# Layer norms with weight and bias as two fused VectorE operations, and gating issued two pairs ahead of its projection

## The chip, the cores and the metric

The kernel runs on one core of one Trainium2 chip. The metric is the device time of one execution in microseconds (us); smaller is better. A core has five engines that the profile names PE (TensorE; its weight loads are PEld), DVE (VectorE), ACT (ScalarE), POOL (GpSimd) and SP (SyncE, which here issues all DMAs). Each engine works through its own instruction list in order and waits where an operand, or the place for a result, is not ready.

## The reference

A two-layer backbone over 1024 latent tokens and 256 context tokens, 1024 features, all in float32. The last layer drops the context tokens, so layer 0 works on ten tiles of 128 tokens and layer 1, in the parts that matter here, on eight.

```
def layer_norm(x, g=None, b=None):
    mu = mean(x, -1); var = mean((x - mu)**2, -1)
    y = (x - mu) * rsqrt(var + 1e-5)
    return y if g is None else y * g + b
# one layer, with shifts, scales and gates from the conditioning vector:
u  = layer_norm(x) * (1 + scale0) + shift0
y  = four mixers of u @ w_in, each group-normed and gated
x1 = layer_norm(ALPHA * x + gate0 * (y @ w_out), ln1_g, ln1_b)
u2 = layer_norm(x1) * (1 + scale1) + shift1
x  = layer_norm(ALPHA * x1 + gate1 * conv_ffn(u2), ln2_g, ln2_b)
```

## The kernel before

Activations for a product lie feature-major in SBUF as two parts, `k.uh` (rounded) and `k.ul` (the rest); `mm3` (L1018 to L1024) makes one product out of three matmuls (L1021 to L1023). A layer runs the four mixers, then `mix_out`, then `ffn`.

`mix_out` (L1127) goes over pairs of token tiles in the order 2, 4, 0, 6, 8 (layer 1: 2, 4, 0, 6). `prep(g0)` gates one pair: DMAs bring the mixers' outputs `yt` and gates `gt` (L1137, L1140), PE transposes them (L1145), ACT and DVE scale and gate them into `yT` (L1148, L1149, L1153), ACT writes `k.uh` (L1156) and POOL `k.ul` (L1157). `out(t)` then does one tile: 48 matmuls with `wo` into two PSUM banks, DVE applies the mixer's gate and adds the residual (`mt`, L1165, L1166), `norm_out` (L1199) normalizes with weight `rg` and bias `rb` into `xt` and stores it, `ln_apply` (L991) normalizes again without weight or bias, and `to_u` (L998) transposes (L1004), modulates (`tum`, L1007 on DVE, L1008 on ACT) and writes `k.uh` on ACT (L1009) and `k.ul` on POOL (L1010) for the feed-forward part. In the loop, `prep` of the next pair is written just ahead of the two `out` of the current one. The last pair uses DVE where the others use POOL.

A layer norm with weight and bias (`norm_out`) is: `ln_stats` (L979; DVE bn_stats and bn_aggr, L983 and L984, a square root on ACT, L985, a reciprocal on DVE, L986, and the product -mean*rstd on DVE, L987), one pass on ACT (L995), the product with the weight (L1204) and the sum with the bias (L1205). In `mix_out` both of these are on POOL; at the end of `ffn` (L1278) the product is on DVE and the sum on POOL.

At the end of `ffn` (L1269 to L1281) each token tile gets its last product in two banks; the second half is added into `facc` (L1277), `norm_out` makes the layer's output from the first bank and that half, and in layer 0 `next_u` (L1266) makes the input of layer 1 with `ln_apply` and `to_u`.

The instruction lists are not in the order of the code: the tile framework schedules with its own timeline, so a change of an operation can move others on every engine.

Of the kernel before, what the change touches and what calls it, by code (L numbers as in the profile page):

```python
# [10 lines left out]
F32=mybir.dt.float32  # L11
# [3 lines left out]
ALU=mybir.AluOpType  # L15
# [5 lines left out]
def rwkv_consts():  # L21
    c={}
# [5 lines left out]
    c['rwmask']=np.stack([mf,mb],1)          # [128,2,128]  # L28
# [10 lines left out]
def mr_consts():  # L39
# [3 lines left out]
    mk=np.zeros((128,2,128),np.float32)   # [j,dir,i]  # L43
    mk[:,0]=np.where(i[:,None]>i[None,:],-1e30,0); mk[:,1]=np.where(i[:,None]<i[None,:],-1e30,0)
    c['mmask']=mk
    # selection for token-major gathers: rows 0-7 wi, 32-39 wk, 64-71 em ; cols (dir,12)
# [5 lines left out]
    # decay broadcast: lhsT [8,(ft,dir),128]  # L52
# [5 lines left out]
    # block-diagonal rows [8 rows,(dir) , h', i]  # L58
# [26 lines left out]
def dft_consts(L):  # L85
    """two-stage real DFT of length 2L, n=128*n1+n2, k=R*m+r, R=2L/128"""
# [10 lines left out]
    F0=np.zeros((128,4,64))   # re0, reH, im0(row0=nyquist), imH  # L97
    F0[:,0]=np.cos(a0);F0[:,1]=np.cos(aH);F0[:,2]=-np.sin(a0);F0[:,2,0]=(-1.0)**n2;F0[:,3]=-np.sin(aH)
    I0=np.zeros((128,4,128))  # B0 from re, B0 from im, BH from re, BH from im
# [36 lines left out]
class Eng:  # L136
    """elementwise ops on DVE or on Pool"""
    def __init__(s,nc,pool): s.nc=nc; s.e=nc.gpsimd if pool else nc.vector; s.pool=pool
    def tt(s,out,a,b,op): s.e.tensor_tensor(out=out,in0=a,in1=b,op=op)
    def axpy(s,out,a,sc,b,op=ALU.add,tmp=None):   # a*sc op b  # L140
# [5 lines left out]
def stage_a(K,E,x,H,CW,ptag):  # L146
    """x: view [128,H,CW] (n1 = token tile). returns accessor re(r), im(r) for r=0..H"""
# [29 lines left out]
def fwd_slot(K,cs,dst_re,dst_im,slot,H,pre,pim,qre=None,qim=None):  # L177
    """matmuls of one slot: re part from (pre,pim), im part from (qre,qim)"""
# [10 lines left out]
def fft_conv(K,Ksp,x,out,H,CW):  # L189
    """x view [128,H,CW], Ksp DRAM AP [128,H,2,CW]; out callback(par(0/1), AP [128,H//2,CW] time values)"""  # L190
# [18 lines left out]
    BB=p.tile([128,2*H,CW],F32,tag="hE",name="BB")   # re r -> r (0..H), im r -> H+r  # L209
# [20 lines left out]
    # g: [128, comp(re,im), r, par, CW]  # L230
# [10 lines left out]
    # a4: even +re B4, odd -im B4  # L241
# [14 lines left out]
def hyena_filter(K,l,L,Ksp):  # L256
    """Ksp DRAM tile [2 order][128,H,2,256]"""
# [89 lines left out]
def seg_conv(k,dst,src,w,ctx=True):  # L347
    """three-tap conv of a padded feature-major tile; w = (prev, mid, next, bias) columns"""
# [18 lines left out]
def kparts(k,D,ft,t,kk):  # L367
    """keys (or normalized keys) to the groups of wrk: r | k of even heads, kk of odd ones | the other way round | kk"""
# [7 lines left out]
def rwkv_front(k,l,pv,pvr,last):  # L376
    """projections, token shift, key normalization, gate and bonus of the RWKV group"""
# [52 lines left out]
def rwkv(K,l,pv,last,p1,p2,p3):  # L430
    """Chunked scan, 64 tokens a chunk, both directions at once, two chunks of each a step.  Even heads keep (b,SA,S) on partitions
    0-63 and (k,V) on 64-127, odd heads the other way round."""
# [610 lines left out]
def later(k,fn=None):  # L1043
    """what follows a projection on the tensor engine is put behind the next projection"""
    p,k.pend=k.pend,fn
    if p: p()
# [398 lines left out]
```

## Time and profile before

| | |
|---|---|
| Time, median of 3 runs | 4327.93 us (4318.99 to 4331.74) |
| Span of the profiled execution | 4332.8 us |
| Median against that span | 4.9 us less |
| `mix_out` in layer 0, layer 1 | 1242 to 1422, 3424 to 3578 us |
| End of `ffn` in layer 0, layer 1 | 2304 to 2404, 4286 to 4333 us |

The profiled execution has no time of its own beside its span; the span lies 1.1 us above the slowest of the three runs. Sums of this text are made against the span, and the 4.9 us are taken off at the end. The stretches in the table are read from the timeline: from the first matmul with `wo` to the last `k.uh` that the feed-forward part waits for, and from the first bn_stats of the last norm to the last `tum` of layer 0, or to the end of the program.

### The profile page before, as it was taken

The numbers are of one execution on the slowest core, as the hardware profiler recorded it, in microseconds if no ns is written. First come the engines' busy times: TensorE is split into PE (matmuls) and PEld (weight loads), VectorE is DVE, ScalarE is ACT, GpSimd is POOL, SyncE is SP. The second block draws the span as 40 slices with busy tenths as digits, with TensorE's granted clock in tenths as the row PEclk, the third lists the DMA queues.
The fourth block names the chain that finished last, engine by engine and source line by source line (L and its number), as shares of the span: only waits on it lengthen the run. The fifth ranks groups of instructions, "written<-read, shape, count | busy, mean of one in ns | idle before, by whom it ended". The sixth has DMA issues, their size and how long they took to land.

```text
span 4332.8 us, 65427 instructions
## 1 busy us (share of the span) xinstructions
PE 3976.9 (92%) x24976; PEld 3226.9 (74%) x24976; DVE 2644.4 (61%) x5384; ACT 1462.4 (34%) x2909; POOL 1094.6 (25%) x2204
## 2 busy tenths in 40 slices
PE   6999999689979999999996899997899879999997
PEld 3878877566657888888884688885666758888885
DVE  5656665889766544444448555776889664444446
ACT  4333233554344211111124443344544342112112
POOL 3230023566535000000033330033666340000004
PEclk6999999799989999999998999996899789999999
DMA  4235553444343111111113235553333331111112
GB/s 164 72 102 173 158 152 110 114 145 121 116 134 122 45 39 35 44 40 35 38 36 114 83 103 153 171 160 96 123 111 102 125 102 54 45 43 54 44 49 97
DMA packets 477141, 414.18 MB, mean 96 GB/s; under 512 B 48827, under 2 KB 443285, under 8 KB 474011
## 3 DMA queue, kind: packets, MB, share of 16 engines
q1 hardware_dynamic: 476826, 409.99, 31.1%
q8 instruction: 197, 3.23, 0.3%
q14 instruction: 118, 0.96, 0.1%
HBM read 323.65 MB, written 86.25 MB: 95 GB/s over the span
## 4 chain that ended last, share of the span: by engine, by line
PE 49%; DVE 11%; ACT 3%; issue 3%; DMA 3%; POOL 3%; SPq 0%; POOLq 0%; ACTq 0%; DVEq 0%
PE bank L1021 8%; PE bank L1023 8%; PE bank L1022 8%; PE dbank L1021 6%; PE dbank L1022 6%; PE dbank L1023 6%; DMA xt<-x 1%; DVE bst L983 1%; POOL ul L1157 1%; DVE facc L1204 1%; PE bank L186 1%; PE bank L187 0%; DMA wst<-in_w_out 0%; DVE G L530 0%; DVE XL L558 0%
## 5 line engine op out<-in xcount | busy, mean ns | idle before, releaser
L1021 PE MATMUL dbank<-uh,wh 128*128 128x512 f32 (+1 forms) x2120 | 764.4, 370 | 9.5 <-ACT tmpB L398 5.5
L1022 PE MATMUL dbank<-ul,wh 128*128 128x512 f32 (+1 forms) x2120 | 760.0, 368 | 0.0
L1015 DVE TENSOR_TENSOR wl<-wst,wh 128x1024 fp32r<-128x1024 f32 x146 | 188.9, 1295 | 491.4 <-ACT wh L1014 342.0
L1023 PE MATMUL dbank<-uh,wl 128*128 128x512 f32 (+1 forms) x2120 | 480.9, 367 | 0.0
L1021 PEld LDWEIGHTS dbank<-uh,wh 128*128 128x128 f32 x2120 | 401.1, 189 | 85.8 <-ACT ztok L1113 6.1
L1022 PEld LDWEIGHTS dbank<-ul,wh 128*128 128x128 f32 x2120 | 401.3, 189 | 68.4 <-issue 0.8
L1023 PEld LDWEIGHTS dbank<-uh,wl 128*128 128x128 f32 x2120 | 366.2, 188 | 70.6 <-issue 1.1
L1232 POOL MEMSET fz<- 128x1 f32 x132 | 7.3, 99 | 1441.4 <-DVE fc L1247 1441.2
L1021 PE MATMUL bank<-uh,wh 128*128 128x512 f32 (+1 forms) x920 | 337.8, 375 | 11.4 <-ACT uh L1009 11.4
L1263 DVE TENSOR_TENSOR facc<-facc,bank 128x512 f32<-128x512 f32 x324 | 222.1, 687 | 204.8 <-PE bank L1023 204.8
L1022 PE MATMUL bank<-ul,wh 128*128 128x512 f32 (+1 forms) x920 | 337.9, 375 | 4.1 <-POOL ul L1010 3.6
L1021 PE MATMUL bank<-wdh,gh 128*128 128x512 f32 x792 | 315.2, 400 | 19.2 <-DVE facc L1277 11.1
L1022 PE MATMUL bank<-wdl,gh 128*128 128x512 f32 x792 | 310.5, 392 | 3.4 <-DVE wdl L1015 3.4
L1023 PE MATMUL bank<-wdh,gl 128*128 128x512 f32 x792 | 248.7, 393 | 0.0
L1014 ACT ACTIVATE wh<-wst 128x1024 fp32r<-128x1024 f32 x146 | 154.6, 1059 | 226.2 <-PE dbank L1022 157.7
L1014 ACT ACTIVATE wdh<-wst 128x1024 fp32r<-128x1024 f32 x46 | 48.7, 1061 | 524.8 <-PE bank L1023 427.8
L557 POOL TENSOR_TENSOR lt<-LM,XL 128x48 f32<-128x48 f32 (+26 forms) x620 | 187.4, 302 | 121.7 <-ACT XL L551 51.1
L558 POOL TENSOR_TENSOR XL<-XL,lt 128x48 f32<-128x48 f32 (+26 forms) x620 | 205.9, 332 | 47.8
L1023 PE MATMUL bank<-uh,wl 128*128 128x512 f32 (+1 forms) x920 | 212.6, 373 | 0.0
L1021 PEld LDWEIGHTS bank<-uh,wh 128*128 128x128 f32 x920 | 176.2, 192 | 42.9 <-ACT uh L1009 12.2
L1022 PEld LDWEIGHTS bank<-ul,wh 128*128 128x128 f32 x920 | 176.0, 191 | 36.1 <-POOL ul L1010 4.3
L1021 PEld LDWEIGHTS bank<-wdh,gh 128*128 128x128 f32 x792 | 149.9, 189 | 59.2 <-DVE facc L1277 11.9
(480 smaller groups left out, 8283.0 us busy)
## 6 DMA issues: line engine op xcount, KB each, us to landing
wst<-in_ffn_w_up SPq DMA_DIRECT2D x88, 512.0 KB
adaw<-in_ada_w SPq DMA_DIRECT2D x160, 256.0 KB
wst<-in_w_in SPq DMA_DIRECT2D x58, 512.0 KB
wst<-in_ffn_w_down SPq DMA_DIRECT2D x46, 512.0 KB
df<-in_c_F SPq DMA_DIRECT2D x10, 1344.0 KB
xt<-x SPq DMA_DIRECT2D x26, 512.0 KB
df<-in_c_I SPq DMA_DIRECT2D x8, 1344.0 KB
rkk<-wrk SPq DMA_DIRECT2D x10, 1024.0 KB
```

Source lines behind the costliest of these rows:

```text
L186: mm(dst_re,F[:,i],pre(slot),start=True,stop=False); mm(dst_re,F[:,i+1],pim(slot),start=False,stop=True)
L557: e.tensor_tensor(out=t_,in0=LM[:,j,j+1:32].unsqueeze(2).to_broadcast([128,n,m]),in1=X[h][:,j:j+1,0:m].to_broadcast([128,n,m]),op=A.mult)
L558: e.tensor_tensor(out=X[h][:,j+1:32,0:m],in0=X[h][:,j+1:32,0:m],in1=t_,op=A.add)
L983: for h in range(2): nc.vector.bn_stats(out=st[:,h],in_=x[h])
L1014: k.nc.scalar.activation(out=h,in_=st,func=ACTF.Copy)
L1015: k.nc.vector.tensor_tensor(out=lo,in0=st,in1=h,op=ALU.subtract)
L1021: mm(ps,lh,rh,start=(i==0),stop=False)
L1022: mm(ps,lh,rl,start=False,stop=False)
L1023: for i,((lh,ll),(rh,rl)) in enumerate(pairs): mm(ps,ll,rh,start=False,stop=(i==n-1 and more is None))
L1157: nc.gpsimd.tensor_tensor(out=k.ul[:,fs,c],in0=yT,in1=k.uh[:,fs,c],op=ALU.subtract)
L1204: e[0].tensor_tensor(out=y,in0=y,in1=g,op=ALU.mult)
L1263: else: tt(out=d,in0=d,in1=ps,op=ALU.add)
```

## The change

`norm_out` no longer calls `ln_apply`. `ln_stats` returns rstd and the mean themselves, without L987, and two operations on DVE do the rest: (x - mean) * weight, and that times rstd plus the bias. At the end of `ffn` the first of them is split in two halves, since the first half of the tile still lies in PSUM. ACT's pass and POOL's two operations are gone from every such norm, and so is the choice of engine. `prep` is called for two pairs ahead of the loop, and in the loop for the pair after the next. Comments were taken out as well, and one line was added, so that line numbers from L987 on are higher by one in the changed kernel.

```
-def ln_stats(k,x):
+def ln_stats(k,x,raw=False):
...
     nc.vector.reciprocal(out=mv[:,2:3],in_=mv[:,2:3])
+    if raw: return mv[:,2:3],mv[:,0:1]
     nc.vector.scalar_tensor_tensor(out=mv[:,3:4],in0=mv[:,0:1],scalar=-1.0,in1=mv[:,2:3],op0=ALU.mult,op1=ALU.mult)
...
-            norm_out(k,t,m,xt,bc['g'],bc['b'],D['x1'],eng)
+            norm_out(k,t,m,xt,bc['g'],bc['b'],D['x1'])
...
-        prep(order[0])
+        prep(order[0]); prep(order[1])
...
-            if i+1<len(order): prep(order[i+1])
-            else: ep.close()
+            if i+2<len(order): prep(order[i+2])
+            elif i+2==len(order): ep.close()
...
-def norm_out(k,t,x,y,g,b,dst,eng=None):
-    nc=k.nc
-    ln_apply(k,y,x)
-    e=eng if isinstance(eng,tuple) else (eng or nc.gpsimd,)*2
-    e[0].tensor_tensor(out=y,in0=y,in1=g,op=ALU.mult)
-    e[1].tensor_tensor(out=y,in0=y,in1=b,op=ALU.add)
+def norm_out(k,t,x,y,g,b,dst):
+    nc=k.nc; stt=nc.vector.scalar_tensor_tensor; hs=[slice(h*512,h*512+512) for h in range(2)]
+    parts=isinstance(x,list)
+    r,m=ln_stats(k,x if parts else [x[:,h] for h in hs],True)
+    for o,i,gg in zip([y[:,h] for h in hs],x,[g[:,h] for h in hs]) if parts else [(y,x,g)]: stt(out=o,in0=i,scalar=m,in1=gg,op0=ALU.subtract,op1=ALU.mult)
+    stt(out=y,in0=y,scalar=r,in1=b,op0=ALU.mult,op1=ALU.add)
     nc.sync.dma_start(dst[t*128:t*128+128],y)
...
-                norm_out(k,t,v,m,g,b,out if last else k.Dn['x'],(nc.vector,nc.gpsimd))
+                norm_out(k,t,v,m,g,b,out if last else k.Dn['x'])
```

On DVE in `mix_out` of layer 0, from the first tile's sum with the residual on, before (`bst` and `bmv` are the statistics, `rm` the gate's row) and then in the changed kernel:

```order
L1166 SCALAR_TENSOR_TENSOR mt<-xt,mt 128x1024
L983 BN_STATS bst<-mt 128x6 x2
L984 BN_AGGR bmv<-bst 128x2
L1165 TENSOR_TENSOR mt<-bank,rm_12708 128x512
L986 RECIPROCAL bmv<-bmv 128x1
L987 SCALAR_TENSOR_TENSOR bmv<-bmv 128x1
L1165 TENSOR_TENSOR mt<-bank,rm_12708 128x512
L1166 SCALAR_TENSOR_TENSOR mt<-xt,mt 128x1024
L983 BN_STATS bst<-xt 128x6 x2
L983 BN_STATS bst<-mt 128x6 x2
L984 BN_AGGR bmv<-bst 128x2 x2
```

```order
L1167 SCALAR_TENSOR_TENSOR mt<-xt,mt 128x1024
L983 BN_STATS bst<-mt 128x6 x2
L984 BN_AGGR bmv<-bst 128x2
L1166 TENSOR_TENSOR mt<-bank,rm_12755 128x512
L1205 SCALAR_TENSOR_TENSOR xt<-mt,bmv,rg 128x1024
L986 RECIPROCAL bmv<-bmv 128x1
L1154 TENSOR_TENSOR yT<-yT,gt 128x512
L1206 SCALAR_TENSOR_TENSOR xt<-xt,bmv,rb 128x1024
L983 BN_STATS bst<-xt 128x6 x2
L984 BN_AGGR bmv<-bst 128x2
L986 RECIPROCAL bmv<-bmv 128x1
L988 SCALAR_TENSOR_TENSOR bmv<-bmv 128x1
```

The first tile's norm now follows its statistics at once on DVE, ahead of the second tile's sum with the residual; before, the statistics of its result (bst<-xt) stood behind the second tile's L1166. A gating product of a later pair (L1154) stands between the two fused operations.

On ACT at the same place, behind the gating of the second pair, before and then in the changed kernel:

```order
L985 ACTIVATE bmv<-bmv,eps_74 128x1
L995 ACTIVATE xt<-mt,bmv 128x1024
L985 ACTIVATE bmv<-bmv,eps_74 128x1 x2
L995 ACTIVATE mt<-xt,bmv 128x1024
L995 ACTIVATE xt<-mt,bmv 128x1024
L1008 ACTIVATE tum<-dbank,modc 128x128 x4
L1009 ACTIVATE uh<-tum 128x8x128
L985 ACTIVATE bmv<-bmv,eps_74 128x1 x2
L995 ACTIVATE mt<-xt,bmv 128x1024
L995 ACTIVATE xt<-mt,bmv 128x1024
```

```order
L985 ACTIVATE bmv<-bmv,eps_74 128x1
L1149 ACTIVATE yT<-dbank,pvm_1661 128x256 x4
L1157 ACTIVATE uh<-yT 128x4x256
L985 ACTIVATE bmv<-bmv,eps_74 128x1
L1149 ACTIVATE yT<-dbank,pvm_1661 128x256 x2
L996 ACTIVATE mt<-xt,bmv 128x1024
L1157 ACTIVATE uh<-yT 128x4x256
L985 ACTIVATE bmv<-bmv,eps_74 128x1
L1009 ACTIVATE tum<-dbank,modc 128x128 x4
L1010 ACTIVATE uh<-tum 128x8x128
```

ACT's passes into xt are gone, and the gating of the third pair (yT and uh<-yT) has moved up to the first two tiles' norms; before, its first rows came only behind the second tile's `tum`.

On DVE at the end of layer 1, where the last eight tiles are normed, from the first tile's statistics on, before and then in the changed kernel:

```order
L984 BN_AGGR bmv<-bst 128x2
L983 BN_STATS bst<-facc 128x6
L986 RECIPROCAL bmv<-bmv 128x1
L984 BN_AGGR bmv<-bst 128x2
L987 SCALAR_TENSOR_TENSOR bmv<-bmv 128x1
L983 BN_STATS bst<-bank 128x6
L986 RECIPROCAL bmv<-bmv 128x1
L987 SCALAR_TENSOR_TENSOR bmv<-bmv 128x1
L1277 TENSOR_TENSOR facc<-facc,bank 128x512
L1204 TENSOR_TENSOR facc<-facc,ln_g 128x1024
L983 BN_STATS bst<-facc 128x6
L1204 TENSOR_TENSOR facc<-facc,ln_g 128x1024
```

```order
L984 BN_AGGR bmv<-bst 128x2
L983 BN_STATS bst<-facc 128x6
L1205 SCALAR_TENSOR_TENSOR facc<-bank,bmv,ln_g 128x512
L1205 SCALAR_TENSOR_TENSOR facc<-facc,bmv,ln_g 128x512
L986 RECIPROCAL bmv<-bmv 128x1
L984 BN_AGGR bmv<-bst 128x2
L983 BN_STATS bst<-bank 128x6
L1206 SCALAR_TENSOR_TENSOR facc<-facc,bmv,ln_b 128x1024
L1205 SCALAR_TENSOR_TENSOR facc<-bank,bmv,ln_g 128x512
L1205 SCALAR_TENSOR_TENSOR facc<-facc,bmv,ln_g 128x512
```

Each tile has three fused operations in place of one product, the reciprocal stands behind the first two of them, and nothing of the norm is left on POOL.

## Rows read from the trace of the kernel before

**Rows 1.** The page: busy us of each engine (share of the span) and instructions.
```profile
PE 3976.9 (92%) x24976; PEld 3226.9 (74%) x24976; DVE 2644.4 (61%) x5384; ACT 1462.4 (34%) x2909; POOL 1094.6 (25%) x2204
```

**Rows 2.** Busy time by stretch: us, busy per engine (instructions), PEclk, DMA share, GB/s.
```profile
1242.00:1422.00 180.00, 161.39 (x719) 129.01 (x719) 117.24 (x203) 82.57 (x136) 85.99 (x37) 0.94 0.37 120
2304.00:2404.00 100.00, 59.57 (x235) 38.42 (x233) 82.68 (x168) 58.10 (x103) 45.17 (x23) 0.78 0.27 93
3424.00:3578.00 154.00, 125.30 (x546) 98.95 (x547) 93.38 (x164) 65.41 (x107) 67.24 (x29) 0.90 0.35 113
4286.00:4332.00 46.00, 21.64 (x78) 13.90 (x76) 36.97 (x57) 13.45 (x24) 18.83 (x8) 0.82 0.23 92
```

**Rows 3.** PE's waits, 1242 to 1422: us in total, times, longest.
```profile
PE bank L1021 <- ACT uh L1156: 29.1, 6, 20.3
```

**Rows 4.** PE's waits, 3420 to 3580, same columns.
```profile
PE bank L1021 <- ACT uh L1156: 12.4, 5, 4.2
```

**Rows 5.** Timeline of PE, both layers: start, us, instruction [idle before].
```profile
1242.30 0.77 PE L1021 MATMUL bank<-wo,uh 128*128 128x512 f32 x1 [20.34 <-ACT uh L1156]
...
1280.51 1.03 PE L1004 MATMUL dbank<-ident,mt 128*128 128x128 f32 x8
...
1415.23 1.09 PE L1004 MATMUL dbank<-ident,mt 128*128 128x128 f32 x8 [1.28 <-ACT mt L995]
...
3463.16 1.04 PE L1004 MATMUL dbank<-ident,mt 128*128 128x128 f32 x8
...
3571.18 1.09 PE L1004 MATMUL dbank<-ident,mt 128*128 128x128 f32 x8 [1.29 <-ACT mt L995]
```

**Rows 6.** Groups by line on DVE, 1266 to 1390: busy us, mean ns | idle before.
```profile
L1166 DVE SCALAR_TENSOR_TENSOR mt<-xt,mt 128x1024 f32<-128x1024 f32 x8 | 17.6, 2199 | 0.1
L1153 DVE TENSOR_TENSOR yT<-yT,gt 128x512 f32<-128x512 f32 x9 | 12.1, 1350 | 3.7 <-ACT yT L1148 3.6
...
L1165 DVE TENSOR_TENSOR mt<-bank,rm 128x512 f32<-128x512 f32 x16 | 10.5, 683 | 12.3 <-PE bank L1023 12.3
...
L987 DVE SCALAR_TENSOR_TENSOR bmv<-bmv 128x1 f32<-128x1 f32 x15 | 8.7, 600 | 0.2
```

**Rows 7.** Timeline of DVE around the projection of layer 0.
```profile
1265.75 0.16 DVE L987 SCALAR_TENSOR_TENSOR bmv<-bmv 128x1 f32<-128x1 f32 x1
...
1294.74 0.69 DVE L1153 TENSOR_TENSOR yT<-yT,gt 128x512 f32<-128x512 f32 x1
1295.35 3.38 DVE L1166 SCALAR_TENSOR_TENSOR mt<-xt,mt 128x1024 f32<-128x1024 f32 x1
...
1318.93 1.23 DVE L1166 SCALAR_TENSOR_TENSOR mt<-xt,mt 128x1024 f32<-128x1024 f32 x1
...
1399.08 1.22 DVE L1204 TENSOR_TENSOR xt<-xt,rg 128x1024 f32<-128x1024 f32 x1
```

**Rows 8.** Groups by line on POOL, 1242 to 1422.
```profile
L1157 POOL TENSOR_TENSOR ul<-yT,uh 128x1024 fp32r<-128x1024 f32 x10 | 24.9, 2494 | 32.5 <-ACT uh L1156 32.5
L1010 POOL TENSOR_TENSOR ul<-tum,uh 128x1024 fp32r<-128x1024 f32 x8 | 21.1, 2642 | 20.1 <-ACT uh L1009 12.0 <-DVE mt L1165 8.1
L1205 POOL TENSOR_TENSOR xt<-xt,rb 128x1024 f32<-128x1024 f32 x8 | 21.1, 2635 | 0.5
L1204 POOL TENSOR_TENSOR xt<-xt,rg 128x1024 f32<-128x1024 f32 x8 | 19.1, 2383 | 30.5 <-ACT xt L995 30.5
```

**Rows 9.** Groups by line on DVE, 2304 to 2404.
```profile
L1204 DVE TENSOR_TENSOR facc<-facc,ln_g 128x1024 f32<-128x1024 f32 x10 | 17.7, 1770 | 4.8 <-ACT facc L995 4.8
...
L987 DVE SCALAR_TENSOR_TENSOR bmv<-bmv 128x1 f32<-128x1 f32 x20 | 8.3, 439 | 0.1
...
L1277 DVE TENSOR_TENSOR facc<-facc,bank 128x512 f32<-128x512 f32 x10 | 6.7, 669 | 0.7 <-PE bank L1023 0.7
```

**Rows 10.** Timelines of DVE and of POOL at the end of layer 1.
```profile
4285.96 0.69 DVE L983 BATCH_NORM_STATS2 bst<-bank 128x6 f32<-128x512 f32 x1
...
4326.79 2.34 POOL L1205 TENSOR_TENSOR facc<-facc,ln_b 128x1024 f32<-128x1024 f32 x1 [2.93 <-DVE facc L1204]
```

## The prediction

> **What bounds the kernel now.** I read the page first, then the four stretches where the changed lines run, then the waits and the timelines inside them. On the page PE is busy 92% of the span [rows 1], so a change on DVE, ACT and POOL can only win where PE waits for them. That leaves some 356 us of the 4332.8 without PE work. By stretch [rows 2]: in `mix_out` PE is idle 180 - 161.39 = 18.6 us in layer 0 and 154 - 125.30 = 28.7 us in layer 1, and the granted clock falls to 0.94 and 0.90, below the upper of its two levels (2.4 GHz), behind such waits. At the end of `ffn` PE is idle 40 of 100 us in layer 0 while DVE is busy 82.68, and in layer 1 DVE is busy 36.97 of 46. So `mix_out` is PE's stage with holes in it, and both ends of `ffn` are DVE's.
>
> The holes in `mix_out`: PE waits 29.1 us for the gating's `uh` in layer 0, of which 20.3 is one wait ahead of the first tile, for the load of `wo`; that one stays [rows 3]. In layer 1 it waits 12.4 for the same (4.2 ahead of the first tile) [rows 4]. What this makes of a tile is seen from the transposes of `mt`, one group a tile: in layer 0 the first starts at 1280.51 and the tenth at 1415.23, nine steps of 14.97 us; in layer 1 3463.16 and 3571.18, seven steps of 15.43. The first projection starts at 1242.30, so the first tile takes 38.2 us to come back [rows 5]. I use these paces as the measure, because every engine's waits end in them.
>
> **How DVE and POOL hinder each other.** The same sum L1166 takes 1.23 us at 1318.93 and 3.38 at 1295.35 [rows 7]; its mean is 2.20 over eight, L1153's 1.35 against 0.69 alone, and that of L987, 128 elements in all, 0.60 against 0.16 [rows 6, 7]. L1165, which reads PSUM, has no such spread (mean 0.68) [rows 6]. The stalls in that stretch sum to 8 x 0.97 + 9 x 0.66 + 15 x 0.44 = 20.3 us over eight tiles, 2.5 a tile. The only thing on POOL there is 128x1024 operations of 2.4 to 2.6 us, 34 in the stage, 30 of which start between 1266 and 1390 by the timeline [rows 8]. So one POOL operation costs DVE s = 20.3 / 30 = 0.68 us on average; the longest stall is 3.38 - 1.23 = 2.15.
>
> **The change, part by part.**
>
> *Fused norm in mix_out.* Away go, per tile, ACT's pass, POOL's 2.38 and 2.64 us [rows 8] and DVE's L987. New are two fused operations on DVE, of one form with L1166 (128x1024, both tensors in SBUF), so 1.23 us each; that the scalar now comes from a tile I take as free, and the product on DVE at 1399.08 has 1.22 too [rows 7]. DVE's work for a tile without stalls is now 117.24 / 10 - 2.5 = 9.2 us [rows 2]; it becomes 9.2 + 2.46 - 0.16 = 11.5. To it come the stalls of what stays on POOL, ten L1157 and eight L1010 [rows 8], 1.8 a tile: 11.5 + 1.8 s. With s as measured that is 12.7 us; if every POOL operation held DVE for its whole 2.4 us it would be 15.8. More of DVE's operations can now be caught (five full-width ones a tile in place of three), so I take s = 1.17: a pace of 13.6. Layer 1 has the same work a tile. PE needs less than that: 161.39 busy us for ten tiles, some of it at the lower clock and some of it feed-forward matmuls already.
>
> *Head start.* The first tile's way has POOL's 5.0 us and ACT's 1.2 replaced by 2.5 us of DVE, and in the new order its second statistics no longer stand behind the second tile's sum. That is 4 to 8 us for each layer; I take 6.
>
> *Gating two pairs ahead.* This adds no instruction; it moves DMA loads, transposes, ACT's and DVE's share of a pair up by one pair, as ACT's new order shows. The waits it can take away are 29.1 - 20.3 = 8.8 and 12.4 - 4.2 = 8.2 us. They are part of the paces above, so I don't count them again; without this part the pace of 13.6 would not be reached, since PE would still stop for `uh` once a pair. `yt` and `gt` have one buffer each, so a pair's loads wait for the transposes and products of the pair before; the loads stand ahead of the residual's `xt` on SP's queue, which costs nothing as long as those transposes are done early.
>
> So layer 0 gains 9 x (14.97 - 13.6) + 6 = 18 and layer 1 7 x (15.43 - 13.6) + 6 = 19. Bounds: at 12.7 they gain 26 and 25, at 15.8, with the head start kept, layer 0 loses 1.5 and layer 1 gains 3.4.
>
> *End of ffn, layer 0.* DVE's 82.68 us hold 11 us of stalls in L1204 and L987 (10 x 0.54 + 20 x 0.28) [rows 9]. Per tile one product of 1.2 and one L987 go, two halves of 0.67 (priced as L1277, one PSUM operand [rows 9]) and one full operation of 1.23 come; counting from start to start, some 0.08 less each, that is 82.7 - 11 - 12.6 + 23.3 = 82.4, say 83. Ten POOL operations remain of twenty: + 10 s. DVE's idle time, 17.3 us now, loses the 4.8 for ACT's pass [rows 9] and some of the waits for transposes: I take 8. That is 83 + 11.7 + 8 = 102.7 against 100: 3 us lost. With s = 0.68 it is 2 gained, with 2.4 15 lost.
>
> *End of ffn, layer 1.* Nothing is left on POOL, so no stalls. A tile costs DVE 0.6 (L1277), 1.2 (statistics), 0.2 and the fused 2.35, 4.4 us in all; eight make 35 from 4285.96, to 4321. Now the last POOL sum ends at 4326.79 + 2.34 = 4329.1 [rows 10]. The square root hides behind the first two fused operations, as the order has it. I take 7.5 us gained, with 5 as the bound if the last tile's chain is not covered.
>
> Sum: 18 + 19 - 3 + 7.5 = 41.5. 4332.8 - 41.5 = 4291.3 of span, less the 4.9 by which the median lies below it: **4286 us**. Rows of layer 1's filters and scans between 2404 and 3424 move too, by the scheduler; that I take as nothing, within 10 us either way.
>
> **The rivals.**
> (1) *The lead does nothing*: with single buffers the loads of the pair after the next wait as before, and the pace stays near 15. Left are the head starts and the ends, 12 + 7.5 - 3 = 16.5: 4311. For it speaks that the waits for `uh` are short ones, (12.4 - 4.2) / 4 = 2 us each in layer 1 [rows 4], against it that the new order has ACT gate the third pair before the first tile's `tum`. Chance 0.13.
> (2) *DVE is full*: the end of layer 0 gets work where DVE is the bound. With s = 2.4 there and idle time of 12.5 it takes 83 + 24 + 12.5 = 119.5, so 20 us are lost in place of 3: 41.5 - 17 = 24.5 gained, 4303. For it speaks DVE's 82.68, against it that half of POOL's work there goes. Chance 0.14. The Trainium skill, Perfetto Trace Analysis, section "Optimizing Scalar/DVE Operations", says that if DVE is saturated, offloading some work to Scalar or even GpSimd may make sense; the change does the reverse, and by that rule this stretch should get longer. The same passage adds that DVE and GpSimd share a port, so that moving work between those two might not help; the stalls above agree.
> (3) *Given back elsewhere*: PE's idle time outside the four stretches is 356 - 112 = 244 us. If the moved rows of layer 1 add a sixth to it, 41 us, nothing is left: 4327. Nothing in the trace of before speaks for that size. Chance 0.12.
> (4) *Slower*: each subtraction left on POOL catches DVE and holds it for its whole length, s = 2.4. Then `mix_out` runs at 15.8, 9 x 0.83 + 7 x 0.37 = 10 lost, the end of layer 0 loses 15, the end of layer 1 gains 7.5, and the head starts shrink from 12 to 2.4, since two operations of each first tile are held as well: 10 + 15 - 7.5 - 2.4 = 15 lost, 4343. It decides from s of about 2.2, more than the longest single stall shown. Chance 0.06. The Trainium skill, SBUF — State Buffer, section "SBUF: two separate sides", calls the pair of ports that DVE and GpSimd share an exclusive lock, held for the whole instruction by the one that comes first, against DVE operations with two SBUF inputs; by that rule a stall of a whole POOL operation is what a DVE operation meets at worst. The rows agree with its kind (3.38 against 1.23, and no spread with a PSUM input), not with that size as a mean.
>
> **How the numbers follow.** The forecast has 0.55, with its own range from 4267 (s = 0.68, and all the rest as above) to 4303. 0.3% of the median, about what a measurement of this kernel can tell from no change, is 13 us: faster is below 4315, slower above 4341. Faster: 0.55 + 0.13 + 0.14 = 0.82; same: 0.12; slower: 0.06. The range of eight in ten goes from 4260, a little below the lower bound for the moved rows, to 4318, which takes in rivals 1 and 2 and leaves out most of 3 and all of 4.
>
> **What the profile of the changed kernel would show.** Transposes of `mt` every 13 to 14 us in both layers, the first of them some 6 us sooner after the first projection; waits for `uh` by L1156 (then L1157) in `mix_out` near the first tile's alone; fused operations of 1.2 us with stalled ones up to 3.5 on full-width rows, none on the halves from PSUM; DVE over 90% busy from the first statistics to the last `tum` of layer 0, in 98 to 107 us; the last store issued about 35 us after the first statistics of layer 1's end, with POOL silent. The prediction is wrong if s comes out at 2 or more, if PE still waits for `uh` once a pair, or if the stretch from the end of layer 0 to layer 1's first projection (2404 to 3424, 1020 us) changes by more than 10 us.

## The result, and the profile after

The changed kernel takes 4260.59 us (median of 4 runs, 4256.27 to 4269.9) against 4323.46 us for the kernel before: a ratio of 0.9859, 95% interval 0.9839 to 0.9879. A second set of six runs (e5) gave 4258.01 us and 0.9843 (0.9818 to 0.9868). So it is faster by 63 us, 1.4 to 1.6%. The forecast was 4286, in a range of 4260 to 4318: the direction is right, but the gain is one and a half times the forecast one, and the time lies at the very edge of the range: 0.6 us inside it in the first set, 2 us outside it in the second.

The page of the changed kernel (answers to [rows 1]): the totals hardly move.

```profile
PE 3956.8 (93%) x24976; PEld 3210.9 (75%) x24976; DVE 2672.2 (63%) x5412; ACT 1416.9 (33%) x2855; POOL 979.7 (23%) x2158
```

The stretches tell more. Busy time in the changed kernel by stretch (columns as in [rows 2]): the steps of `mix_out` in layer 0, the end of `ffn` in layer 0, the steps of layer 1, the end of layer 1.

```profile
1273.00:1387.00 114.00, 114.00 (x546) 93.53 (x545) 105.68 (x171) 52.87 (x93) 32.18 (x16) 1.00 0.37 124
2272.00:2363.00 91.00, 57.76 (x216) 36.71 (x215) 86.83 (x179) 42.96 (x81) 21.16 (x14) 0.79 0.28 97
3426.00:3514.00 88.00, 80.96 (x373) 65.20 (x371) 80.78 (x129) 37.86 (x67) 20.67 (x12) 0.96 0.33 113
4228.00:4268.00 40.00, 21.98 (x76) 15.19 (x76) 36.30 (x65) 2.35 (x8) 0.00 (x0) 0.82 0.26 105
```

The same for the kernel before, cut to the steps of `mix_out`, which the wider stretches of [rows 2] hide:

```profile
1280.50:1415.20 134.70, 121.22 (x548) 96.71 (x546) 96.05 (x167) 65.13 (x108) 69.22 (x31) 0.95 0.35 114
3463.20:3571.20 108.00, 82.87 (x369) 65.12 (x367) 72.28 (x129) 49.58 (x81) 50.43 (x23) 0.89 0.31 103
```

PE is now busy in 114.00 of 114 us of layer 0's steps, at a granted clock of 1.00, and DVE in 105.68. Before, it was 121.22 and 96.05 of 134.7. So in layer 0 it is PE that has no idle time left, while DVE still has 8.3 us. In layer 1 neither is full: PE has 80.96 and DVE 80.78 of 88.

The timeline of PE in the changed kernel, with the marks of [rows 5]: first product with `wo`, first and last transposes of `mt`, in both layers.

```profile
1238.99 0.77 PE L1022 MATMUL bank<-wo,uh 128*128 128x512 f32 x1 [20.66 <-ACT uh L1157]
...
1273.05 1.04 PE L1005 MATMUL dbank<-ident,mt 128*128 128x128 f32 x8
...
1387.29 0.93 PE L1005 MATMUL dbank<-ident,mt 128*128 128x128 f32 x7
...
3390.64 0.80 PE L1022 MATMUL bank<-wo,uh 128*128 128x512 f32 x1 [4.23 <-ACT uh L1157]
...
3425.98 1.04 PE L1005 MATMUL dbank<-ident,mt 128*128 128x128 f32 x8
...
3514.05 1.10 PE L1005 MATMUL dbank<-ident,mt 128*128 128x128 f32 x8 [2.01 <-ACT mt L996]
```

PE's waits there (1230 to 1410, then 3380 to 3530): of the waits for the gating's `uh` [rows 3, 4] only those ahead of the first tile are left, and in layer 1 the second norm's `mt` is what PE now waits for.

```profile
PE bank L1022 <- ACT uh L1157: 20.7, 1, 20.7
...
PE dbank L1005 <- ACT mt L996: 6.4, 3, 3.0
PE bank L1022 <- ACT uh L1157: 4.2, 1, 4.2
```

DVE's groups in 1266 to 1390 (answers to [rows 6]):

```profile
L1167 DVE SCALAR_TENSOR_TENSOR mt<-xt,mt 128x1024 f32<-128x1024 f32 x9 | 15.9, 1766 | 0.2
L1206 DVE SCALAR_TENSOR_TENSOR xt<-xt,bmv,rb 128x1024 f32<-128x1024 f32 x9 | 15.1, 1674 | 0.2
L1205 DVE SCALAR_TENSOR_TENSOR xt<-mt,bmv,rg 128x1024 f32<-128x1024 f32 x9 | 14.6, 1625 | 0.2
...
L1166 DVE TENSOR_TENSOR mt<-bank,rm 128x512 f32<-128x512 f32 x17 | 11.4, 673 | 0.0
L988 DVE SCALAR_TENSOR_TENSOR bmv<-bmv 128x1 f32<-128x1 f32 x10 | 5.3, 531 | 0.2
L1154 DVE TENSOR_TENSOR yT<-yT,gt 128x512 f32<-128x512 f32 x8 | 5.2, 684 | 0.6 <-ACT yT L1149 0.5
```

And what a long one of them stands beside, timelines of DVE and of POOL:

```profile
1280.23 2.98 DVE L1167 SCALAR_TENSOR_TENSOR mt<-xt,mt 128x1024 f32<-128x1024 f32 x1
...
1279.73 2.40 POOL L1011 TENSOR_TENSOR ul<-tum,uh 128x1024 fp32r<-128x1024 f32 x1 [5.74 <-DVE bmv L984]
...
1297.94 3.23 DVE L1206 SCALAR_TENSOR_TENSOR xt<-xt,bmv,rb 128x1024 f32<-128x1024 f32 x1
...
1297.00 3.09 POOL L1158 TENSOR_TENSOR ul<-yT,uh 128x1024 fp32r<-128x1024 f32 x1 [0.25 <-ACT uh L1157]
```

POOL's operation ends at 1282.13; DVE's, alone 1.23 us [rows 7], ends some 1.1 us later (1280.23 + 2.98 = 1283.21). The second pair reads alike: POOL ends at 1300.09, DVE at 1301.17. A stalled operation on DVE has its own work left when POOL's ends. The Trainium skill, SBUF — State Buffer, section "SBUF: two separate sides", tells of a lock held for the whole instruction: these rows agree, in size too. A mean stays below that: of POOL's 14 operations in 1266 to 1390, 11 are followed in this way by the end of a lengthened DVE operation, lengthened by 0.5 to 2.0 us according to how late in POOL's 2.4 us it came, and 3 by none. The hindrance goes both ways, as POOL's 3.09 us in place of 2.40 shows, beside a DVE operation (L1205) that ran until 1297.83.

DVE's groups at the end of layer 0, 2272 to 2363.4 (answers to [rows 9]): the half out of PSUM has no stall (mean 0.74 us), the half out of SBUF has (1.25).

```profile
L1206 DVE SCALAR_TENSOR_TENSOR facc<-facc,bmv,ln_b 128x1024 f32<-128x1024 f32 x10 | 12.7, 1273 | 0.0
L1205 DVE SCALAR_TENSOR_TENSOR facc<-facc,bmv,ln_g 128x512 f32<-128x512 f32 x10 | 12.5, 1252 | 0.0
L1205 DVE SCALAR_TENSOR_TENSOR facc<-bank,bmv,ln_g 128x512 f32<-128x512 f32 x10 | 7.4, 736 | 0.0
...
L988 DVE SCALAR_TENSOR_TENSOR bmv<-bmv 128x1 f32<-128x1 f32 x10 | 3.6, 363 | 0.0
L1274 DVE SCALAR_TENSOR_TENSOR facc<-xt,facc 128x1024 f32<-128x1024 f32 x2 | 3.6, 1794 | 0.0
...
L1016 DVE TENSOR_TENSOR wdl<-wst,wdh 128x1024 fp32r<-128x1024 f32 x2 | 2.4, 1210 | 0.0
L1016 DVE TENSOR_TENSOR wl<-wst,wh 128x1024 fp32r<-128x1024 f32 x1 | 1.2, 1198 | 0.0
```

Layer 1's end, first statistics and last operation on DVE (answers to [rows 10]):

```profile
4228.58 0.69 DVE L983 BATCH_NORM_STATS2 bst<-bank 128x6 f32<-128x512 f32 x1
...
4263.06 1.28 DVE L1206 SCALAR_TENSOR_TENSOR facc<-facc,bmv,ln_b 128x1024 f32<-128x1024 f32 x1
```

The four places as the marks give them, in us. A head is first product with `wo` to first transposes of `mt`; steps are first to last transposes of `mt` (nine and seven); the end of layer 0 is first statistics to last `tum` on DVE, the end of layer 1 first statistics to the last operation on DVE. The rest is the span less these six.

| profiled execution | head 0 | steps 0 | end 0 | head 1 | steps 1 | end 1 | sum | rest |
|---|---|---|---|---|---|---|---|---|
| before | 38.2 | 134.7 | 100.3 | 38.6 | 108.0 | 40.8 | 460.6 | 3872.2 |
| changed | 34.1 | 114.2 | 91.1 | 35.3 | 88.1 | 35.8 | 398.6 | 3869.4 |
| changed, again (e5) | 33.4 | 114.3 | 91.3 | 36.0 | 86.4 | 35.8 | 397.2 | 3849.8 |
| e1 norms alone | 35.6 | 117.9 | 91.3 | 36.1 | 86.4 | 35.8 | 403.1 | 3865.1 |
| e2 lead alone | 41.0 | 126.8 | 98.0 | 41.5 | 97.7 | 40.5 | 445.5 | 3846.3 |
| e3 more on POOL | 34.1 | 131.3 | 91.1 | 35.8 | 91.0 | 35.8 | 419.1 | 3875.8 |
| e4 `tum` on ACT | 35.7 | 113.0 | 86.6 | 33.5 | 85.5 | 35.8 | 390.1 | 3875.8 |
| e6 plain on DVE | 40.0 | 127.0 | 97.4 | 40.9 | 96.7 | 37.7 | 439.7 | 3850.4 |
| e7 before, third `mt` | 39.0 | 129.2 | 97.9 | 39.1 | 95.0 | 40.7 | 440.9 | 3863.5 |
| e8 both halves in PSUM | 34.1 | 114.3 | 81.5 | 36.5 | 86.9 | 33.8 | 387.1 | 3859.5 |
| e9 one-tensor product | 37.0 | 111.4 | 90.8 | 35.1 | 85.0 | 35.8 | 395.1 | 3887.4 |
| e10 three together | 37.3 | 111.4 | 83.4 | 33.7 | 85.2 | 33.8 | 384.8 | 3855.0 |
| e11 third `mt` | 34.0 | 118.0 | 91.2 | 35.5 | 81.5 | 35.8 | 396.0 | 3903.0 |

From before to changed the six places give 62.0 us and POOL's last sum, behind DVE's end in the kernel before, 2.4: 64.4 of the spans' 64.8. The two executions of one kernel agree within 2 us at each place, but their rests differ by 20. So the places are read from single profiles, and times of whole kernels only with their intervals.

Head and steps of a layer belong together. In layer 0 they sum to 148.3 and 147.7 us in the two profiles of the changed kernel, and to 148.4 to 148.7 in e4, e8, e9 and e10, which are the changed kernel with less work on DVE in one place or another: PE has no idle time in the steps of any of these, so that a few us less in the steps are a few more in the head. In layer 1, where PE has idle time, the same sum is 123.4 and 122.4 in the changed kernel, 119.0 in e4, 120.1 in e9, 118.9 in e10.

### The profile page after: what moved, and what is told of

Read it like the earlier page. It is cut to its first block, busy times and chain, and to the rows that moved or that the text cites. A ratio compares the mean times of both kernels' runs of the same rounds, so it can differ in the third digit from the quotient of the medians.

```text
span 4268.0 us, 65334 instructions
## 1 busy us (share of the span) xinstructions
PE 3956.8 (93%) x24976; PEld 3210.9 (75%) x24976; DVE 2672.2 (63%) x5412; ACT 1416.9 (33%) x2855; POOL 979.7 (23%) x2158
## 4 chain that ended last, share of the span: by engine, by line
PE 52%; DVE 11%; DMA 3%; issue 2%; POOL 1%; ACT 1%; SPq 0%; ACTq 0%; DVEq 0%; POOLq 0%
PE bank L1022 9%; PE bank L1023 9%; PE bank L1024 9%; PE dbank L1022 6%; PE dbank L1023 6%; PE dbank L1024 6%; DVE bst L983 1%; DMA xt<-x 1%; DVE facc L1205 1%; PE bank L186 1%; PE bank L187 1%; DMA wst<-in_w_out 1%; PE dbank L529 0%; DVE facc L1206 0%; DVE facc L1274 0%
## 5 line engine op out<-in xcount | busy, mean ns | idle before, releaser
L1015 ACT ACTIVATE wh<-wst 128x1024 fp32r<-128x1024 f32 x146 | 154.8, 1060 | 238.1 <-PE dbank L1023 168.4
L1015 ACT ACTIVATE wdh<-wst 128x1024 fp32r<-128x1024 f32 x46 | 48.8, 1062 | 529.4 <-PE bank L1024 427.7
L1022 PEld LDWEIGHTS bank<-uh,wh 128*128 128x128 f32 x920 | 174.1, 190 | 36.1 <-ACT uh L1010 5.6
```

What stands on the lines that cost most here:

```text
L1015: k.nc.scalar.activation(out=h,in_=st,func=ACTF.Copy)
L1022: mm(ps,lh,rh,start=(i==0),stop=False)
```

## The experiments

Theory A: DVE's work and its stalls behind POOL set the pace of `mix_out` and of the ends of `ffn`; the lead only keeps PE from stopping for `uh`. Theory B: the lead sped `mix_out` up. Theory C: the shorter chain of a tile's norm (the operations that one tile must go through one after the other) did, since `mt` and `xt` have two buffers each.

**e1, the norms alone**

```
-        prep(order[0]); prep(order[1])
+        prep(order[0])
-            if i+2<len(order): prep(order[i+2])
-            elif i+2==len(order): ep.close()
+            if i+1<len(order): prep(order[i+1])
+            else: ep.close()
```

> The changed kernel with gating one pair ahead as before. Theory A (the pace of mix_out is set by VectorE's work and its stalls; the lead only keeps TensorE from stopping for uh): TensorE waits for uh again once a pair, some 8.8 us in layer 0 and 8.2 in layer 1, the ends of ffn stay; about 4278 us. Theory B (the lead is what sped mix_out up, the norms only the ends of ffn): the steps of mt go back to 15.0 and 15.4 us, 20.5 + 20 us lost, about 4301. Theory C (the shorter chain of a tile's norm is what sped mix_out up, since mt and xt have two buffers each): 4261 to 4266, steps still below 13.

Measured: 4267.23 us, ratio 0.9873 (0.9853 to 0.9893), which overlaps the changed kernel's 0.9839 to 0.9879: what the lead adds to the norms is not clear of noise in the whole time. B is out: the steps stay near the changed kernel's. A's loss of 17 is not there either; the six places lose 4.5 to 6 us. C's 4261 to 4266 is the nearest, though its steps below 13 came in layer 1 alone (12.3, and 13.1 in layer 0). PE's waits for `uh` in layer 0, 1240 to 1405:

```profile
PE bank L1022 <- ACT uh L1157: 24.3, 5, 19.9
```

Less the first, 4.4 us in four waits are left of the 8.8 of [rows 3]: PE still stops for each pair's gating, as A has it, but for half as long, although the lead is gone. That the gating comes sooner because the norm's work has left ACT and POOL fits this, and is argued, not shown by itself.

**e2, the lead alone** (the kernel before with the two lines of the lead)

> The kernel before with gating two pairs ahead. Theory A: only the waits for uh go, 17 us, about 4306, steps of mt 14 us or more, since VectorE still stalls behind the norm's two POOL operations. Theory B: steps of 12.7, 40 us gained, about 4283. Theory C: nothing but noise, 4318 to 4328.

Measured: 4303.98 us, ratio 0.9968 (0.9952 to 0.9983), steps of 14.1 and 14.0 us, as A has it. The norms give 1.27% alone, the lead 0.32%, both together 1.41 and 1.57%: additive within the intervals. The places are not additive: the six give 15.1 us for the lead alone, 57.5 for the norms alone, and 62.0 and 63.4 for both, so that the lead is worth 15 us by itself and 4.5 to 6 on top of the norms.

**e3, more on POOL**

```
+            if eng is None:
+                for _ in range(2): nc.gpsimd.tensor_tensor(out=sc,in0=bc['b']...,in1=k.uh[:,:,c],op=ALU.subtract)
```

> The changed kernel with two more POOL subtractions of 128x1024 behind each tile's own in mix_out, into a tile that nobody reads, for eight tiles of layer 0 and six of layer 1: 28 operations of 2.4 us. POOL stays below 80% busy there. Theory A: each costs VectorE a stall of 0.9 us as those of the changed kernel do, and VectorE has 7% idle in that stretch: 28 x 0.9 = 25 us slower, about 4286 (at least 4273 if half of it is covered). Theories B and C: no one waits for the extra operations, within 5 us of 4261.

Measured: 4299.19 us, ratio 0.9946 (0.9932 to 0.996), 38 us or more over the changed kernel. The table parts this: 17.1 us in layer 0's steps and 2.9 in layer 1's, and some 18 in layer 1's feed-forward part, which e11 explains otherwise. Windows of the steps of both layers, then groups on DVE and on POOL in 1269 to 1400 (lines moved by two):

```profile
1269.10:1400.30 131.20, 118.92 (x547) 95.14 (x545) 125.97 (x171) 52.21 (x93) 79.22 (x32) 0.97 0.31 108
3431.80:3522.80 91.00, 69.72 (x326) 54.95 (x324) 86.36 (x126) 34.40 (x63) 57.24 (x24) 0.93 0.22 80
...
L1207 DVE SCALAR_TENSOR_TENSOR xt<-mt,bmv,rg 128x1024 f32<-128x1024 f32 x9 | 19.5, 2172 | 0.2
L1208 DVE SCALAR_TENSOR_TENSOR xt<-xt,bmv,rb 128x1024 f32<-128x1024 f32 x9 | 19.0, 2115 | 0.2
...
L1171 POOL TENSOR_TENSOR sc<-rb,uh 128x1024 f32<-128x1024 f32 x16 | 47.6, 2975 | 0.4
```

Nobody waits for `sc`, yet the fused operations go from 1.63 and 1.67 us to 2.17 and 2.12. DVE's busy time in the steps of layer 0 grows from 105.7 to 126.0 us with 16 more operations on POOL: 1.27 us each, and DVE, with 5.2 us idle of 131.2, is fuller there than PE (118.92). Stalls behind POOL are shown as a cause in layer 0, close to the 1.17 that the prediction took for s. In layer 1, 12 more operations on POOL add 5.6 us to DVE (86.36 against 80.78), 0.5 each, and 2.9 to the steps: what one costs is no constant. The 0.9 of the expectation had the changed kernel's stalls divided among too many operations (see below).

**e4, more of `tum` on ACT**

```
-            if q<(2 if h or tag!="tum" or bufs==1 else 3): nc.vector.tensor_scalar(...
+            if q<1: nc.vector.tensor_scalar(...
```

> The changed kernel with six of the eight 128x128 pieces of tum on ScalarE in place of four, in mix_out and at the end of ffn. VectorE loses 0.7 us a tile, ScalarE gains 0.8. Theory A: faster, 5 us in layer 1's mix_out, 0 to 6 in layer 0's (TensorE is busy all the time there), 5 to 7 at the end of layer 0: 4243 to 4251. Theories B and C: not faster, since nothing in the chain of a tile gets shorter (four pieces one after the other on ScalarE take longer): 4258 to 4268.

Measured: 4273.86 us, ratio 0.9886 (0.987 to 0.9902). The end of layer 0 is 4.5 us shorter, near A's 5 to 7. In layer 0 head and steps together are no shorter, which A allowed (0 to 6); in layer 1 they are by 3.4 to 4.4, near A's 5. The whole is not faster. The edit also reached the first norms of the kernel, which use the same function, so that the rest can have grown by it; whether it did is not settled.

**e6, the norm's two operations plain on DVE** (the kernel before with the lead, `norm_out` given VectorE for both operations)

> The kernel before with gating two pairs ahead and the product and the sum of every norm with weight and bias as two plain operations on VectorE, behind ScalarE's pass; POOL is left as in the changed kernel, and only the fusing is missing. Theory A (VectorE's work and POOL's stalls of it decide): VectorE has the same two operations of 1.2 us, and one of 128 elements and a wait for ScalarE more: 0.3 to 0.6 us a tile in four stretches of 10, 8, 10 and 8 tiles, 11 to 22 us, so 4271 to 4283. Theory C (the shorter chain of a norm decides; ScalarE's pass and its two handovers are back in it): half of the gain of the norms is lost, 4285 or more. Theory D (POOL's absence is all that counts): as the changed kernel, 4258 to 4266.

Measured: 4289.26 us, ratio 0.9917 (0.989 to 0.9944): C's number, and D is out. In `mix_out` moving the two operations from POOL to DVE bought nothing by itself: steps of 127.0 and 96.7, against e2's 126.8 and 97.7 with both on POOL. Window and DVE's waits over the steps of layer 0:

```profile
1284.90:1411.90 127.00, 114.75 (x531) 91.93 (x530) 101.68 (x177) 61.62 (x101) 32.46 (x15) 0.96 0.32 108
...
DVE xt L1204 <- ACT xt L995: 14.1, 9, 2.3
DVE bmv L986 <- ACT bmv L985: 6.1, 7, 1.4
```

DVE is busy less than in the changed kernel, 101.68 against 105.68 us, but waits 14.1 us for ACT's pass into `xt`, nine times, once a tile, and 6.1 for ACT's square root, in an instruction list that goes in order. In the changed kernel the wait for the square root is 1.4 us there, since a fused operation that doesn't need it stands ahead, and the other is gone. This is what theory A left out: beside the plain form on DVE, the fused form takes away DVE's stops for ACT, (14.1 + 6.1 - 1.4) / 9 = 2.1 us a tile, of which 1.4 show in the steps (127.0 against 114.2). In the kernel before, with the two operations on POOL, it was POOL that stood behind ACT's pass [rows 8].

The steps can now be followed one change at a time. Layer 0: 134.7 before, 126.8 with the lead (e2), 127.0 with both operations plain on DVE (e6), 114.2 with them fused. Layer 1: 108.0, 97.7, 96.7, and 88.1 or 86.4. In another order the shares are others: the norms first (e1) give 117.9 and 86.4, and the lead then 3.7 in layer 0 and nothing in layer 1.

**e7, a third `mt` in the kernel before** (`bufs=2` to `bufs=3`)

> The kernel before with three buffers of mt in place of two in mix_out. Theory A: the third buffer hands the engines work earlier, but VectorE's stalls remain: within 8 us of the kernel before, 4312 to 4324. Theory C (chain of a tile over two buffers sets the pace): steps of mt below 14 us, 15 to 25 us gained, 4295 to 4305.

Measured: 4313.73 us, ratio 0.9981 (0.996 to 1.0002): no clear gain, as A has it, but for another reason. The steps went down by 5.5 and 13.0 us, to 14.4 and 13.6 each, so the two buffers did bind in layer 1, as C has it. The feed-forward part of layer 1 gave 18 us back (732.4 us against 714.8, from last transposes of `mt` to first statistics; see e11).

**e8, both halves of the last product left in PSUM**

```
-                mm3(k,v[1],down(t,h[1],gs,wd)); tt(out=m[:,h[1]],in0=m[:,h[1]],in1=v[1],op=ALU.add); v[1]=m[:,h[1]]
+                mm3(k,v[1],down(t,h[1],gs,wd),(k.ident,m[:,h[1]]))
```

> The changed kernel with the second half of the last product too left in PSUM at the end of ffn: TensorE adds the old value with the identity, as it does for the first half, so that VectorE's sum of 0.66 us goes and the second fused half reads PSUM, where no stall is seen. Theory A (VectorE bounds both ends of ffn, 95% and 90% busy): 1.1 us less a tile in layer 0, 0.7 in layer 1, so 9 to 11 and 5 us less: 4244 to 4250, the end of layer 0 in 81 us in place of 91. Rival: TensorE and its banks bound them, with 0.6 us more work a tile and a bank held until the fused operation: 4261 to 4272.

Measured: 4243.31 us, ratio 0.9814 (0.9787 to 0.9842). The ends went from 91.1 to 81.5 and from 35.8 to 33.8. Windows of both ends:

```profile
2270.40:2351.90 81.50, 62.55 (x247) 39.08 (x246) 75.09 (x170) 42.69 (x82) 23.96 (x14) 0.88 0.34 116
4208.90:4242.60 33.70, 27.34 (x97) 17.78 (x95) 33.00 (x57) 2.36 (x8) 0.00 (x0) 0.98 0.27 109
```

DVE bounds the end of layer 0, as A has it (9.6 us of the 9 to 11): its busy time falls from 86.83 to 75.09, about what the sum (L1278, 6.6 us) and the stalls of the half out of SBUF (5.1) came to. At layer 1's end only 2 of 5 came: DVE is busy for 33.00 of 33.70 us there, but PE rises from 21.98 of 40 to 27.34. This version is faster than the kernel before; against the changed kernel of the same hours (0.9843, 0.9818 to 0.9868) the intervals overlap, so that its 15 us less are not clear of noise, and the 11.6 us at the two ends are what the profiles show.

**e9, the product of 128 elements with one tensor**

```
-    nc.vector.scalar_tensor_tensor(out=mv[:,3:4],in0=mv[:,0:1],scalar=-1.0,in1=mv[:,2:3],op0=ALU.mult,op1=ALU.mult)
+    nc.vector.tensor_scalar(out=mv[:,3:4],in0=mv[:,0:1],scalar1=-1.0,scalar2=mv[:,2:3],op0=ALU.mult,op1=ALU.mult)
```

> The changed kernel with the product -mean*rstd (L988, 128 elements) as a tensor_scalar with the mean as its one tensor and rstd as a per-partition scalar, in place of a scalar_tensor_tensor with two tensors. Theory A with stalls only where an operation reads two tensors from SBUF: the stalled ones of 0.5 to 0.7 us on average in mix_out and 0.36 at the end of layer 0 fall to 0.15, 0.2 to 0.5 us a tile, 6 to 10 us in all: 4249 to 4254. If the stalls fall on whatever VectorE does while POOL works: the mean stays above 0.35, 4256 to 4264.

Measured: 4273.35 us, ratio 0.9885 (0.9862 to 0.9908). Line 988 over the whole execution, in the changed kernel and then in e9 (shortest, median and longest in ns):

```profile
L988 DVE SCALAR_TENSOR_TENSOR bmv<-bmv x38: 93/151/2355, 30.8 to 3512.6; 128x1 f32<-128x1 f32 x38
```

```profile
L988 DVE TENSOR_SCALAR bmv<-bmv x38: 150/203/216, 30.5 to 3526.4; 128x1 f32<-128x1 f32 x38
```

The stalls on it are gone, as A has it: 0.216 us at the longest in place of 2.355. The gain of 6 to 10 us did not come. In layer 0 the steps are 2.8 us shorter and the head 2.9 longer, and in layer 1 both together are 2.3 to 3.3 shorter; the end of layer 0 stays at 90.8. The steps of layer 0, then a group on DVE at the end of layer 0, 2278 to 2368.8:

```profile
1282.75:1394.18 111.43, 111.43 (x536) 91.48 (x535) 101.14 (x168) 51.55 (x92) 31.56 (x15) 1.00 0.36 121
...
L1206 DVE SCALAR_TENSOR_TENSOR facc<-facc,bmv,ln_b 128x1024 f32<-128x1024 f32 x10 | 15.7, 1568 | 0.0
```

In the steps of layer 0 PE is busy throughout, so that relieving DVE gains nothing there. At the end POOL's operations catch another one: L1206 takes 15.7 us in place of 12.7, and DVE is busy for 86.52 us in place of 86.83. Taking one operation out of POOL's way leaves the next one in it.

The median lies 13 to 15 us above the changed kernel's, of other hours, though the interval overlaps that of either set. By the profile this is the rest, 3887.4 us, most of it between the layers (1039.0 us at a granted clock of 0.89, against 1027.2 at 0.90 and 1020.7 at 0.91 in the two profiles of the changed kernel). Why is open: the scheduler orders the mixers of layer 1 anew with each edit.

**e10, three together**

```
-            if q<(2 if h or tag!="tum" or bufs==1 else 3): ...
+            if q<(1 if tag!="tum" else 2 if h or bufs==1 else 3): ...
```

> Three things together: the second half in PSUM too (e8), the one-tensor product (e9), and at the end of layer 0 alone two of eight pieces of tum on VectorE in place of four (the start of the kernel and mix_out keep theirs). Theory A: the end of layer 0 goes from 81.5 to 74 to 77 us, e9's gain in the rest: 4228 to 4238. Rival (with VectorE relieved the end of layer 0 waits for ScalarE's passes and for TensorE): the end stays at 80 or more, 4236 to 4243.

Measured: 4250.52 us, ratio 0.9838 (0.9808 to 0.9868), above both ranges. At the place it is the rival's number: the end of layer 0 stays at 83.4 us. The group of L1206 at this place in e8 (2270.4 to 2351.9), and then in e10 (2273 to 2356.4) DVE's longest wait and the groups of L1206 and of a cast:

```profile
L1206 DVE SCALAR_TENSOR_TENSOR facc<-facc,bmv,ln_b 128x1024 f32<-128x1024 f32 x10 | 12.7, 1269 | 0.0
```

```profile
DVE tum L1008 <- POOL ul L1011: 6.5, 2, 4.1
...
L1206 DVE SCALAR_TENSOR_TENSOR facc<-facc,bmv,ln_b 128x1024 f32<-128x1024 f32 x10 | 18.2, 1816 | 0.0
L1072 DVE CAST wh<-wst 128x128 fp32r<-128x128 f32 x1 | 1.8, 1764 | 0.0
```

The wait for POOL's `ul` is no new one, e8 had 6.0 us of it; for ACT and PE themselves, the rival's reason, DVE waits 2.5 us in all. The work that left DVE came back as stalls: 20 pieces of `tum` took 6.5 us with them and the one-tensor product 1.4, but L1206 is 5.5 us longer than in e8, since POOL's subtractions now catch it (three of the ten end 1.1 us behind one of them), and DVE is busy for 73.81 us against 75.09. The cast, which reads one tensor, took 1.76 us from 2331.46 on, until just behind the end of POOL's operation at 2333.14, and 0.17 in the changed kernel: operations with two tensors are not the only ones that POOL holds up.

**e11, a third `mt` in the changed kernel**

> The changed kernel with three buffers of mt in mix_out. Theory A: VectorE is 92% busy there and TensorE 100% in layer 0, so the steps of mt shorten by less than 0.5 us in layer 1 and not at all in layer 0; and the feed-forward part of layer 1 takes 18 us more, as in both kernels so far that gave mix_out 4 KB a partition more: about 4272 to 4278. Theory C (buffers still bind): steps below 12 us in layer 1. If the 18 us came from something else in those two kernels: 4256 to 4262.

Measured: 4295.83 us, ratio 0.9929 (0.9906 to 0.9952). In layer 0 the steps didn't shorten; they are 3.8 us longer (118.0). In layer 1 they did, to 11.6 us each, C's number: the two buffers still cost 0.7 us a tile or more there, and A's 92% was not the whole. The feed-forward part of layer 1 took 18 us more for the third time, in all three kernels that gave `mix_out` 4 KB a partition more and in no other (732.4 to 732.7 us from last transposes of `mt` to first statistics, against 713.6 to 715.4). PE's waits from the last step on (3520 to 3640), and the load of the part's first weights, here and then in the changed kernel:

```profile
PE bank L1022 <- ACT wh L1015: 9.5, 1, 9.5
PE dbank L1005 <- ACT mt L996: 9.3, 1, 9.3
...
3532.73 1.01 SPq L1030 DMA_DIRECT2D wst<-in_ffn_w_up  x2
```

```profile
3499.61 5.21 SPq L1030 DMA_DIRECT2D wst<-in_ffn_w_up  x2
```

The wait for `mt` is the last step's own; the one for `wh` lies behind it. The weights come late: their load is issued 10.7 us behind the last tile's store (3522.01) and 6.1 behind its transposes (3526.61), in the changed kernel 14.4 us ahead of them (3514.05). That the larger pool holds the room for these loads until it closes fits this, but was not tried by itself.

## Why the prediction was right, and where its terms were off

**Direction and place.** The gain lies where the forecast put it, in `mix_out` and at the ends of `ffn`: 64.4 us at the places, where the sum had 41.5. That the time is still inside the range is luck, by 0.6 us in one set of runs and not at all in the other. Rival 1 (the lead does nothing, the pace stays near 15) falls with the steps of 12.7 us, though it was right that the lead is worth little in the whole time: 0.32% alone, 4267 against 4258 to 4261 us on top of the norms. Rival 2 (DVE full at the end of layer 0) has DVE at 86.83 of 91 us, full as it said, but the stretch got shorter. Rivals 3 and 4 did not come.

**mix_out: 18 and 19 forecast, 24.6 and 23.2 measured.** The heads gave 4.1 and 3.3 in place of 6. The steps went to 12.7 and 12.6 us in place of 13.6. The step that was mis-sized is "DVE's work for a tile without stalls is now 117.24 / 10 - 2.5 = 9.2": those 180 us also hold the work ahead of the first step. From the steps alone it is 96.05 / 9 - 2.5 = 8.2. In the changed kernel DVE is busy 105.68 / 9 = 11.7 a tile; the stalls in its groups are 9 x (0.54 + 0.44 + 0.40) + 10 x 0.37 = 16.1 us over nine tiles, 1.8 a tile, or 1.15 for each of the 14 POOL operations that run in 1266 to 1390 by the timeline, the first of them from 1265.31 (s was taken as 1.17). That leaves 9.9 for the work, where 11.5 was taken, and 0.9 a tile is idle. Of the 1.6 between them 1.0 is the base; the steps also hold the gating of two pairs in place of three (L1154 six times, L1153 nine times before), some 0.3 a tile; 0.3 stays open. The s of 1.17, chosen between 0.68 and 2.4 without a row of its own, came out at 1.15; that is luck as much as judgement.

The mechanism holds in part. The pace was made of DVE's work and stalls; "PE needs less than that" was said of 13.6. In layer 0 it is PE that has no idle time at 12.7 us a tile, and relieving DVE gains nothing there (e4, e9, e10); that 12.7 is also the sum's lower bound is chance. In layer 1 the pace does yield to less work on DVE (e4, e9, e10) and to a third `mt` (e11), so DVE and the two buffers both have a share.

**"Without this part the pace of 13.6 would not be reached"** is wrong: e1 has 13.1 and 12.3 without the lead. Its reason came true, PE does stop for `uh` once a pair, but for 4.4 us in all in layer 0.

**What the sum left out.** It priced ACT's pass in the head alone. e6 shows what it would be in every step, a stop of DVE's list, had the two operations gone to DVE plain: the exchange then gains nothing in the steps, and fused it gains 12.8 us in layer 0 and 8.6 or more in layer 1. That the pass goes too is what made the added work on DVE affordable. And the two buffers of `mt` bound the kernel before in layer 1 (e7), which "every engine's waits end in them" hid.

**End of layer 0: 3 lost forecast, 9.2 gained.** The 82.68 us of [rows 2] also held stalls that the term kept as work, in DVE's splitting of weights (L1015 there took 2.16 and 2.94 us, now 1.21). Of 11.7 for stalls, 5.1 on the fused half out of SBUF, 2.1 on L988 and 1.1 on the residual's sum (1.79 us) are seen; DVE's idle time is 4.2 us in place of 8. So the 11.7 us between 102.7 and 91 are 3.4 of stalls, 3.8 of idle time and 4.5 of work, 3.6 of it those stalls on L1015. (The 12.6 for what goes is 12.0 by the terms that the prediction names; that has no weight.)

**End of layer 1: 7.5 forecast, 7.4 measured**, the square roots hidden as the order had it, POOL silent, and the last operation 35.8 us behind the first statistics, where 35 stood.

**The rest.** Taken as nothing within 10 us: the stretch between the layers' places took 7 us more in one profile of the changed kernel and 0.7 more in the other; 4 us went in layer 0's feed-forward part (888.9 to 884.9 us from last transposes of `mt` to first statistics, PE idle 9.5 of them before and 5.8 after). That is within what two executions of one kernel differ by.

## What to carry to other kernels

Where an engine works its list in order, price an edit by what the list stops for as well as by its work: two operations more on DVE were cheap because a handover to ACT and back went with them, while the same two behind the handover gained nothing in `mix_out`. Ask again, at the new pace, which engine has no idle time: in layer 0 that was no longer the one that the sum was made for, and relieving DVE further bought nothing. Take the base of a pace from the steps alone, marked by an event that comes once a tile, and not from a stretch around them. POOL's elementwise work is not free beside a busy DVE: each operation on it cost 1.15 to 1.27 us of DVE's time in layer 0's steps and 0.5 in layer 1's (e3), almost all of it on operations that read two tensors from SBUF, and an operation taken out of its way left another in it (e9, e10).

## What had not been expected of the hardware

A product of 128 elements with two tensors takes up to 2.36 us on DVE while POOL works, and 0.22 at most when its second operand is a per-partition scalar (e9). A stalled operation ends at a set distance behind POOL's, by its size: some 1.1 us for 128x1024, 0.55 for 128x512 (a fused half, 2295.38 to 2298.08, POOL to 2297.53), 0.01 for 128x1 (L988, 2334.88 to 2336.99, POOL to 2336.98). And two executions of one kernel differed by 21 us of span with every one of the six places equal within 2 us. The scatter lies for the most part in what precedes each `mix_out`, the mixers: between the layers PE is idle nearly as long (95.2 and 93.0 us) but busy 932.11 and 927.76 us, at a granted clock of 0.90 and 0.91, and ahead of layer 0's `mix_out` it is busy 1092.19 and 1081.22 us at 0.91 and 0.92; over all kernels the clock between the layers went from 0.89 (e9, e11) to 0.93 (e10).
